# Three pieces of x moved from SyncE's DMA queue to ScalarE's at the start of a decoder block

## The chip, the cores and the metric

The kernel runs on one core of a Trainium2 chip. The time is the device time of one execution in microseconds (us), the median of several runs; less is better. A profile is one execution recorded by the hardware profiler. The engines are named as the profile names them: PE (TensorE matmuls, with its weight loads as PEld), DVE (VectorE), ACT (ScalarE), POOL (GpSimd) and SP (SyncE, which here only issues DMAs; its issues have the name SPq).

## The reference

One decoder block over 256 tokens of width 1024, in float32, in outline:

```python
u = rmsnorm(h, norm_mix_pre)
z = u @ w_in                      # 4096 columns: pool, q, k, v, two gates
y_pool = pool_mixer(p, pool_w, pool_scale) @ w_branch_pool
y_attn = moba_attention(q, k, v) @ w_branch_attn
m = sigmoid(g_pool) * y_pool + sigmoid(g_attn) * y_attn
h = h + rmsnorm(m @ w_out, norm_mix_post)
u2 = rmsnorm(h, norm_mlp_pre)
a = square(relu(u2 @ w_up))       # 4096 columns
h = h + rmsnorm(a @ w_down, norm_mlp_post)
```

What matters here is the very beginning: x has to be loaded and turned, and the first product that is made of it is the values, v = u @ w_in[:, 1536:2048].

## The kernel before, in words

Every float32 product is made of three matmuls (`mm3`, lines 232 to 234): each operand is split into a high part in fp32r and a low part, the rounding that is left, and high times high, low times high and high times low are summed in PSUM. So each block of a weight is first loaded raw (`Block.load`, line 80), then split: ACT copies it to the high part (`split_hi`, line 89), and DVE and POOL subtract to get the low part (line 93; `share_lo` gives DVE 352 of 512 columns and POOL 160). The order of the instructions on every engine is that of the program text; nothing reorders them.

The first stage makes the values. Its weight has eight pieces v_r of 128 rows and 512 columns (256 KB each), called piece 0 to piece 7 below; x has four pieces x(t, n) of 256 KB, where t is the half of the tokens (two halves of 128) and n the half of the 1024 columns. All are loaded over SP's queue, interleaved as line 202 and the lines behind it say:

```python
load_x(0, 0); g_mix.load(); load_v(0); load_v(1)
load_x(1, 0); load_v(2); load_x(0, 1); load_v(3); load_x(1, 1)
for k in range(4, KD): load_v(k)
```

PE turns a piece of x by four transposes (`turn_x`, line 322); ACT makes the high part uh of 128 columns of it (line 329) and DVE the low part ul (line 330). `v_rows(t, k)` is the three matmuls of piece k of the weight with half t of the tokens; there are 16 such triples. On PE they stand in this order: turn x(0,0), nine small matmuls that only keep the engine busy, v_rows(0,0), turn x(1,0), v_rows(0,1), v_rows(1,0), turn x(0,1), v_rows(1,1), v_rows(0,2), v_rows(1,2), turn x(1,1), and then the two halves of pieces 3 to 7. Piece 0 has its high part made by DVE (the CAST of line 375), pieces 1 to 7 by ACT.

Behind the values come q, k, the pool projection, the scores, the gates and the rest; their weights are all loaded over SP's queue, in three raw buffers.

ACT's first two instructions are the load of its function table and a one-column activation `warm` (line 67) that asks for it; then it waits for the first turned piece of x.

Of the kernel before, what the change touches and what calls it, by code (L numbers as in the profile page):

```python
# [16 lines left out]
P = 128  # L17
# [3 lines left out]
KD = D // P  # L21
# [12 lines left out]
def hybrid_block(ctx: ExitStack, tc: tile.TileContext, x, norm_mix_pre, w_in, b_gate, pool_w, pool_scale,  # L34
# [4 lines left out]
    nc = tc.nc  # L39
# [110 lines left out]
    def load_next():  # L150
        if done[0] < len(order):
            order[done[0]].load_all()
            done[0] += 1
# [12 lines left out]

    x_sb = act.tile([P, NT, D], F32, name="x_sb")

    def load_x(t, n):
        c = slice(n * 512, (n + 1) * 512)  # L170
        nc.sync.dma_start(x_sb[:, t, c], x[0, t * P:(t + 1) * P, c])


    class Columns:
# [24 lines left out]
    def load_v(k):  # L199
        bv[k // 4].load(k % 4)  # L200

    load_x(0, 0)
    g_mix.load()
    load_v(0)
    load_v(1)
    load_x(1, 0)
    load_v(2)
    load_x(0, 1)
    load_v(3)
    load_x(1, 1)  # L210
    for k in range(4, KD):
        load_v(k)
    load_next()
    others.load()

# [760 lines left out]
```

## Time and profile before

| | |
|---|---|
| median of 3 runs | 340.37 us (340.05 to 341.89) |
| the profiled execution's own time | 339.66 us |
| its span, from the first to the last instruction | 337.9 us |
| outside the span (339.66 less 337.9) | 1.76 us |
| PE busy | 329.9 us, 98% of the span |
| DVE, ACT, POOL busy | 220.3, 182.2 and 77.9 us |
| HBM read | 61.10 MB |

The time of an engine counts what it does, not whether anything waits for it. The chain of waits is followed back from the last instruction of the program, at each step to what released it; what lies on it set the end. All times of rows are counted from the start of the span.

### The profile page before, as it was taken

Reading aid. Unit: us, or ns where it says so; the run is one execution under the profiler, and the core shown is the slowest. Engines: PE = TensorE matmul, PEld = TensorE weight load, DVE = VectorE, ACT = ScalarE, POOL = GpSimd, SP = SyncE. Lnnn points to the kernel's source line nnn. Section 1 sums busy time; section 2 is a strip of 40 time slices with the busy share of each in tenths; the row PEclk is TensorE's granted clock in tenths of the full one; section 3 lists DMA queues with packets and bytes.
Section 4 is the critical chain, followed back from the end, with each engine's and each line's share of the span. In section 5 each row is a group of like instructions: output and inputs, shape, how many; then the busy total and the mean of one; then the engine's idle time right before and its main releaser. Section 6 shows DMA issues by size and latency. Waiting matters only on the chain.

```text
span 337.9 us, 5701 instructions
## 1 busy us (share of the span) xinstructions
PE 329.9 (98%) x2325; PEld 305.0 (90%) x2325; DVE 220.3 (65%) x292; ACT 182.2 (54%) x256; POOL 77.9 (23%) x68
## 2 busy tenths in 40 slices
PE   8999999999999999999999999999999999999992
PEld 7799999999999999888898998989989989899881
DVE  3899777998385789376686746637366374653535
ACT  3984678665837755175768436354263551544331
POOL 3698589155305000056600000000000000000000
PEclk9999999999999999999999999999999999999999
DMA  6996971644555946707355854907629267090003
GB/s 211 375 324 216 222 232 27 237 151 140 209 189 207 353 135 240 248 4 248 124 176 198 288 211 139 330 30 263 236 74 317 109 236 262 11 353 14 0 0 124
DMA packets 27363, 63.04 MB, mean 187 GB/s; under 512 B 1317, under 2 KB 2761, under 8 KB 27337
## 3 DMA queue, kind: packets, MB, share of 16 engines
q1 hardware_dynamic: 26760, 62.15, 53.4%
q0 software_dynamic: 576, 0.52, 1.2%
q8 instruction: 18, 0.29, 0.4%
q14 instruction: 9, 0.07, 0.1%
HBM read 61.10 MB, written 1.05 MB: 184 GB/s over the span
## 4 chain that ended last, share of the span: by engine, by line
PE 96%; DMA 1%; DVE 1%; SPq 0%; DVEq 0%; ACT 0%; issue 0%; ACTq 0%
PE up_ps L232 9%; PE up_ps L234 9%; PE up_ps L233 9%; PE d_ps L242 7%; PE d_ps L241 7%; PE d_ps L245 7%; PE g_ps L232 4%; PE g_ps L233 4%; PE g_ps L234 4%; PE wo_ps L241 2%; PE wo_ps L242 2%; PE wo_ps L245 2%; DMA x_sb<-in_x_dram 1%; PE q_ps L232 1%; PE p_ps L234 1%; PE q_ps L234 1%
## 5 line engine op out<-in xcount | busy, mean ns | idle before, releaser
L232 PE MATMUL up_ps<-u2h,up_h 128*128 128x256 f32 x224 | 62.1, 277 | 0.0
L233 PE MATMUL up_ps<-u2l,up_h 128*128 128x256 f32 x224 | 61.9, 276 | 0.0
L234 PE MATMUL up_ps<-u2h,up_l 128*128 128x256 f32 x224 | 61.9, 276 | 0.0
L93 DVE TENSOR_TENSOR dn_l<-dn_r,dn_h 128x2048 fp32r<-128x2048 f32 x16 | 36.5, 2292 | 16.4 <-ACT dn_h L89 16.3
L233 PEld LDWEIGHTS up_ps<-u2l,up_h 128*128 128x128 f32 x224 | 42.1, 188 | 0.0
L232 PEld LDWEIGHTS up_ps<-u2h,up_h 128*128 128x128 f32 x224 | 42.1, 188 | 0.0
L241 PE MATMUL d_ps<-dn_h,ah 128*128 128x512 f32 x108 | 42.1, 389 | 0.0
L242 PE MATMUL d_ps<-dn_l,ah 128*128 128x512 f32 x108 | 42.1, 389 | 0.0
L234 PEld LDWEIGHTS up_ps<-u2h,up_l 128*128 128x128 f32 x224 | 42.1, 188 | 0.0
L89 ACT ACTIVATE dn_h<-dn_r 128x2048 fp32r<-128x2048 f32 x16 | 30.4, 1915 | 21.2 <-issue 12.8
L892 POOL TENSOR_TENSOR o_out<-o_out,g_mlp_post 128x256 f32<-128x256 f32 x1 | 0.7, 737 | 159.1 <-ACT o_out L891 159.1
L232 PE MATMUL g_ps<-uh,g_h 128*128 128x256 f32 x128 | 35.6, 278 | 0.0
L93 DVE TENSOR_TENSOR up_l<-up_r,up_h 128x2048 fp32r<-128x2048 f32 (+1 forms) x14 | 30.2, 2193 | 8.1 <-ACT up_h L89 8.1
L233 PE MATMUL g_ps<-ul,g_h 128*128 128x256 f32 x128 | 35.3, 276 | 0.0
L234 PE MATMUL g_ps<-uh,g_l 128*128 128x256 f32 x128 | 35.3, 276 | 0.0
L245 PE MATMUL d_ps<-dn_h,al 128*128 128x512 f32 x108 | 33.2, 389 | 0.0
L805 ACT ACTIVATE relu<-up_ps 128x512 f32<-128x512 f32 x16 | 9.5, 597 | 39.4 <-PE up_ps L234 39.4
L89 ACT ACTIVATE up_h<-up_r 128x2048 fp32r<-128x2048 f32 x16 | 29.9, 1904 | 1.6 <-PE wo_ps L245 1.6
L807 DVE TENSOR_TENSOR a<-up_ps,relu 128x512 f32<-128x512 f32 x16 | 11.0, 690 | 28.9 <-ACT relu L805 28.8
L93 POOL TENSOR_TENSOR up_l<-up_r,up_h 128x640 fp32r<-128x640 f32 (+1 forms) x4 | 15.6, 3914 | 44.2 <-ACT up_h L89 44.2
L245 PEld LDWEIGHTS d_ps<-dn_h,al 128*128 128x128 f32 x108 | 20.3, 188 | 4.2
L233 PEld LDWEIGHTS g_ps<-ul,g_h 128*128 128x128 f32 x128 | 24.0, 188 | 0.0
(240 smaller groups left out, 858.0 us busy)
## 6 DMA issues: line engine op xcount, KB each, us to landing
up_r<-in_w_up_dram SPq DMA_DIRECT2D x16, 1024.0 KB, 5.6
dn_r<-in_w_down_dram SPq DMA_DIRECT2D x16, 1024.0 KB, 4.9
g_r<-in_w_in_dram SPq DMA_DIRECT2D x8, 1024.0 KB, 5.5
o_r<-in_w_out_dram SPq DMA_DIRECT2D x4, 1024.0 KB, 5.0
v_r<-in_w_in_dram SPq DMA_DIRECT2D x8, 256.0 KB, 5.4
q_r<-in_w_in_dram SPq DMA_DIRECT2D x4, 512.0 KB, 6.3
k_r<-in_w_in_dram SPq DMA_DIRECT2D x2, 1024.0 KB, 5.9
p_r<-in_w_in_dram SPq DMA_DIRECT2D x2, 1024.0 KB
```

The costliest lines, as they stand in the source:

```text
L89: nc.scalar.activation(self.hi[:, s, :], self.raw[:, s, :], AF.Copy)
L93: eng.tensor_tensor(self.lo[:, s, c], self.raw[:, s, c], self.hi[:, s, c].bitcast(F32), ALU.subtract)
L232: nc.tensor.matmul(ps, wh, rh, start=start, stop=False, skip_group_check=True)
L233: nc.tensor.matmul(ps, *second, start=False, stop=False, skip_group_check=True)
L234: nc.tensor.matmul(ps, *third, start=False, stop=stop, skip_group_check=True)
L241: nc.tensor.matmul(ps, xh, wh[:, c], start=start, stop=False, skip_group_check=True)
L242: nc.tensor.matmul(ps, xh, wl[:, c], start=False, stop=False, skip_group_check=True)
L245: nc.tensor.matmul(ps, xl, wh[:, c], start=False, stop=stop, skip_group_check=True)
L805: nc.scalar.activation(r, ps, AF.Relu)
L807: nc.vector.tensor_tensor(a, ps, r, ALU.mult)
L892: nc.gpsimd.tensor_tensor(o[:, 768:D], o[:, 768:D], g_mlp_post[:, 768:D], ALU.mult)
```

## The change

`load_x` is given the queue that it issues on. The first piece of x stays on SP's queue, the eight pieces of the weight follow it there without a break, and the other three pieces of x are issued by ACT, in the order x(1,0), x(0,1), x(1,1).

```diff
-    def load_x(t, n):
+    def load_x(t, n, queue):
         c = slice(n * 512, (n + 1) * 512)
-        nc.sync.dma_start(x_sb[:, t, c], x[0, t * P:(t + 1) * P, c])
+        queue.dma_start(x_sb[:, t, c], x[0, t * P:(t + 1) * P, c])
...
-    load_x(0, 0)
+    load_x(0, 0, nc.sync)
     g_mix.load()
-    load_v(0)
-    load_v(1)
-    load_x(1, 0)
-    load_v(2)
-    load_x(0, 1)
-    load_v(3)
-    load_x(1, 1)
-    for k in range(4, KD):
+    for k in range(KD):
         load_v(k)
+    for t, n in ((1, 0), (0, 1), (1, 1)):
+        load_x(t, n, nc.scalar)
     load_next()
     others.load()
```

Five lines fewer stand ahead of what follows, so a line of the kernel before has a number smaller by five after it (329 becomes 324).

SP's issues at the start of the program, before. x_sb are the pieces of x, v_r those of the weight; DMAHW0 to DMAHW7 are eight semaphores that the loads take in turn (x(0,0) has 0, g_mix 1, piece 0 has 2, piece 1 has 3, x(1,0) has 4, piece 2 has 5, x(0,1) has 6, piece 3 has 7), so that the ninth load waits until the first has landed.

```order
L80 DMA v_r<-in_w_in_dram 128x512 x2
L171 DMA x_sb<-in_x_dram 128x512
L80 DMA v_r<-in_w_in_dram 128x512
L171 DMA x_sb<-in_x_dram 128x512
L80 DMA v_r<-in_w_in_dram 128x512
L171 DMA x_sb<-in_x_dram 128x512 [waits DMAHW0_49]
L80 DMA v_r<-in_w_in_dram 128x512 [waits DMAHW1_49]
L80 DMA v_r<-in_w_in_dram 128x512 [waits DMAHW2_49]
L80 DMA v_r<-in_w_in_dram 128x512 [waits DMAHW3_49]
L80 DMA v_r<-in_w_in_dram 128x512 [waits DMAHW4_49]
L80 DMA q_r<-in_w_in_dram 128x2x512 [waits DMAHW5_49]
L80 DMA q_r<-in_w_in_dram 128x2x512 [waits DMAHW6_49]
```

The last two rows are the first two loads of q's weight. Pieces 4 to 7 are the four rows ahead of them.

The same place on SP after the change, where x(1,0), x(0,1) and x(1,1) hold the semaphores 3, 5 and 7, and pieces 1 to 4 hold 4, 6, 0 and 1:

```order
L171 DMA x_sb<-in_x_dram 128x512
L184 DMA g_mix_row<-in_norm_mix_pre_dram 8x128
L80 DMA v_r<-in_w_in_dram 128x512 x3
L80 DMA v_r<-in_w_in_dram 128x512 [waits DMAHW0_49]
L80 DMA v_r<-in_w_in_dram 128x512 [waits DMAHW1_49]
L80 DMA v_r<-in_w_in_dram 128x512 [waits DMAHW2_49]
L80 DMA v_r<-in_w_in_dram 128x512 [waits DMAHW3_49]
L80 DMA v_r<-in_w_in_dram 128x512 [waits DMAHW4_49]
L80 DMA q_r<-in_w_in_dram 128x2x512 [waits DMAHW5_49]
L80 DMA q_r<-in_w_in_dram 128x2x512 [waits DMAHW6_49]
```

Three issues have left SP; piece 3 now waits for x(0,0), piece 5 for piece 0, piece 6 for x(1,0) and piece 7 for piece 1.

ACT at the start of the program after the change, from its table load to the second weight piece that it splits:

```order
L67 ACT_TABLE_LOAD
L67 ACTIVATE warm<-eps 128x1 [waits DVE_49]
L171 DMA x_sb<-in_x_dram 128x512 x3
L324 ACTIVATE uh<-x_ps_164,g_mix_col 128x128 [waits DVE_49,PE_49]
L324 ACTIVATE uh<-x_ps_164,g_mix_col 128x128 [waits DVE_49]
L89 ACTIVATE v_h<-v_r 128x512 [waits DMAHW4_49]
L324 ACTIVATE uh<-x_ps_188,g_mix_col 128x128 [waits PE_49]
L324 ACTIVATE uh<-x_ps_188,g_mix_col 128x128 [waits DVE_49]
L89 ACTIVATE v_h<-v_r 128x512 [waits DMAHW6_49]
```

The three issues stand between `warm` and the first uh and wait for nothing of their own; the rest of ACT's order is as before.

## Rows read from the trace of the kernel before

**Rows 1.** The page: the span, and busy time, share and instructions of each engine.
```profile
span 337.9 us, 5701 instructions
...
PE 329.9 (98%) x2325; PEld 305.0 (90%) x2325; DVE 220.3 (65%) x292; ACT 182.2 (54%) x256; POOL 77.9 (23%) x68
```

**Rows 2.** The page: the chain that ended last, share of the span by engine.
```profile
PE 96%; DMA 1%; DVE 1%; SPq 0%; DVEq 0%; ACT 0%; issue 0%; ACTq 0%
```

**Rows 3.** The same chain in order of time, 0 to 20 us: start, length, what.
```profile
2.46 4.58 DMA x_sb<-in_x_dram
7.09 0.66 PE x_ps L322 x4
...
10.61 0.36 PE v_ps L233
...
12.33 0.23 PE v_ps L232
...
18.98 0.23 PE v_ps L234
```

**Rows 4.** Windows: stretch, then busy us of PE, PEld, DVE, ACT, POOL; clock, DMA share, GB/s.
```profile
1.50:2.00 0.50, 0.50 (x7) 0.50 (x6) 0.00 (x0) 0.50 (x1) 0.50 (x3) 1.00 0.27 102
0.00:3.35 3.35, 2.57 (x24) 2.48 (x24) 0.06 (x1) 1.49 (x2) 1.82 (x10) 1.00 0.39 119
5.00:6.00 1.00, 1.00 (x9) 0.68 (x7) 1.00 (x3) 0.58 (x3) 0.53 (x1) 1.00 0.90 285
12.00:13.00 1.00, 1.00 (x8) 0.86 (x6) 0.69 (x3) 0.63 (x2) 0.59 (x1) 1.00 1.07 410
20.00:330.00 310.00, 310.00 (x2219) 289.31 (x2218) 203.30 (x252) 167.02 (x224) 66.36 (x48) 1.00 0.53 181
```

**Rows 5.** Timeline of SP's issues: start, length, engine, line, what.
```profile
0.74 0.38 SPq L171 DMA_DIRECT2D x_sb<-in_x_dram  x1
2.46 0.43 SPq L171 DMA_DIRECT2D x_sb<-in_x_dram  x1
...
7.06 0.33 SPq L80 DMA_DIRECT2D v_r<-in_w_in_dram  x1
7.83 1.54 SPq L80 DMA_DIRECT2D q_r<-in_w_in_dram  x2
8.99 0.38 SPq L80 DMA_DIRECT2D q_r<-in_w_in_dram  x1
9.66 0.30 SPq L184 DMA_DIRECT2D others_row<-in_norm_mlp_pre_dram  x1
10.33 0.28 SPq L184 DMA_DIRECT2D others_row<-in_pool_scale_dram  x1
```

**Rows 6.** Timeline of ACT, 0 to 20 us.
```profile
2.03 0.20 ACT L67 ACTIVATE warm<-eps 128x1 f32<-128x1 f32 x1
4.78 0.37 ACT L329 ACTIVATE uh<-x_ps,g_mix_col 128x128 fp32r<-128x128 f32 x1 [2.55 <-PE x_ps L322]
...
5.83 0.62 ACT L89 ACTIVATE v_h<-v_r 128x512 fp32r<-128x512 f32 x1
...
15.70 3.93 ACT L89 ACTIVATE q_h<-q_r 128x1024 fp32r<-128x1024 f32 x4
```

**Rows 7.** Timelines of DVE, POOL and PE, 4.7 to 8.3 us, around pieces 0 and 1.
```profile
4.77 0.43 DVE L375 CAST v_h<-v_r 128x512 fp32r<-128x512 f32 x1 [0.86 <-DMA v_r<-in_w_in_dram]
...
6.53 0.86 POOL L93 TENSOR_TENSOR v_l<-v_r,v_h 128x160 fp32r<-128x160 f32 x1 [0.72 <-ACT v_h L89]
...
6.33 0.47 PE L234 MATMUL v_ps<-v_l,uh 128*128 128x512 f32 x1 [0.24 <-DVE v_l L93]
...
7.82 0.40 PE L233 MATMUL v_ps<-v_l,uh 128*128 128x512 f32 x1
```

**Rows 8.** The page's DMA issues: KB each, us to landing; POOL's own issues, in ns.
```profile
q_r<-in_w_in_dram SPq DMA_DIRECT2D x4, 512.0 KB, 6.3
...
L485 POOL DMA_DIRECT2D stacked<-stacked x4: 581/586/817, 32.3 to 36.2; - x4
```

## The prediction

> **What bounds the kernel now.** I read the page first: PE is busy for 98% of the span of 337.9 us [rows 1], and 96% of the chain that ended last is PE, 1% a DMA [rows 2]. So the question is what PE waits for, and where. The windows answer it: from 20 to 330 us PE is busy for 310.00 of 310.00 us [rows 4]. A delay or a gain ahead of 20 us therefore goes to the end undiminished, and nothing that happens to the transfers of x can save more than what PE loses before that.
>
> The chain in order of time shows the loss. It begins with the load of x(1,0), issued at 2.46 us, 4.58 us until it has landed at 7.04; PE turns it at 7.09 [rows 3]. From there it is PE without a hole, but for one matmul that took 0.36 us in place of 0.23 at 10.61; from 12.33 to the start of the last at 18.98 stand 30 matmuls at 0.23 each [rows 3]. PE had started the matmul before that wait at 6.33 [rows 7] and could have gone on 0.23 later, at 6.56. So at this place 7.09 - 6.56 = 0.53 us are to be had, with the 0.13 at 10.61 together 0.66 us: **0.2% of the time, the most that any order of landing gives** while piece 0 of the weight, at the head of its queue, lands at 4.77 [rows 7]. What can be lost has no such limit.
>
> I call "same" what lies within 0.5% of 340.37, that is 1.7 us; a measurement of this kernel can hardly tell less from no change. Durations come from the profiled execution, whose time of 339.66 us is 0.71 below the median; I add the differences to the median.
>
> **When the loads land now.** An issue on SP that waits for a semaphore shows when an earlier load landed. The issue at 7.06 waited for x(1,0), that at 7.83 for piece 2, at 8.99 for x(0,1), at 9.66 for piece 3, at 10.33 for x(1,1) [rows 5]; piece 0 landed at 4.77. Counting x(0,0) as the first, the second load landed at 4.77, the fourth at 7.04, the fifth to eighth at 7.83, 8.99, 9.66 and 10.33. Six loads of 256 KB in 5.56 us are 0.93 us each. The DMA engines are the limit here, at 285 GB/s and a share of 0.90 from 5 to 6 us; later they move 410 [rows 4].
>
> **The change, part by part.**
>
> *Three issues leave SP.* One takes 0.43 us [rows 5]. Piece 2 is issued where x(1,0) was, at 2.46, pieces 3 and 4 sooner than now as well. That alone is worth nothing, since it is the transfers that are slow, and not the issues.
>
> *Three issues come to ACT.* They start when `warm` is done, at 2.03 + 0.20 = 2.23 us, and ACT then stands idle until 4.78 [rows 6], 2.55 us. The trace has no issue on ACT. Its bounds are SP's 0.43 us and the longest of POOL's, 0.82 [rows 8]: 1.3 to 2.5 us for three. I take SP's, the same kind of transfer, so ACT is free at about 3.6; even the upper end ends at 4.7. Cost: nothing, covered by the idle time. Were the cover gone, the first uh would be late by as much as the issues run over, with 0.53 us of slack until x(1,0).
>
> x(1,0) is thus issued at about 2.26 and not 2.46: the table load and `warm` stand ahead of it, and the change **gains 0.2 us of issue, no more**. x(0,1) and x(1,1) gain more, but PE meets them without a wait now.
>
> *What lands when, with two queues.* This decides. x(0,0) was issued at 0.74 [rows 5] and its first bytes came after 1.5, at most 0.05 MB of them by 2.00 [rows 4], so at about 1.8: 1.1 us from issue to bytes. x(1,0), issued at 2.26, can move bytes from about 3.35. By then 119 GB/s x 3.35 us = 0.40 MB have been moved [rows 4], 1.5 loads: x(0,0) and half of piece 0. From there both queues have work all the time. If they share the engines evenly, loads end in this count of loads moved: piece 0 at 2.5 (it was 2), x(1,0) at 3.5 (it was 4), piece 1 at 4.5 (it was 3), x(0,1) at 5.5 (6), piece 2 at 6.5 (5), x(1,1) at 7.5 (8), piece 3 at 8 (7), and from piece 4 on all as before. Between the landings above this reads: piece 0 at 5.34, x(1,0) at 6.47, **piece 1 at 7.44**, x(0,1) 8.41, piece 2 9.33, x(1,1) 10.0, piece 3 10.33.
>
> The trace has nothing of two queues in this stage, so I bound the landing of piece 1: at the low end 5.83, when ACT starts on it now [rows 6], if the loads go on in the order of their issue; at the high end 8.99, as the sixth load, if all of x goes ahead of it. I take 7.44, the even share, which is also the middle.
>
> [...]
>
> *What PE then waits for.* Piece 0 at 5.34 moves the matmul at 6.33 to 6.90 and its end of turn to 7.13, level with the 7.09 of now; x(1,0) is there by then. But v_rows(0,1) needs piece 1 split. From the start of its high part on ACT (5.83) to the end of POOL's share of the low part (6.53 + 0.86 = 7.39) are 1.56 us [rows 6, 7], and the second matmul of that triple started at 7.82 [rows 7], 0.43 later. With piece 1 at 7.44 it starts at 7.44 + 1.56 = 9.00: **+1.18 us**. What is queued behind it on PE, v_rows(1,0), x(0,1) and v_rows(1,1), is ready by then. Piece 2, at 9.33, has its low part at about 10.9, and PE comes to it at about 11.3: no wait, and the 0.13 at 10.61 are saved. Piece 3 has nearly two microseconds to spare. Sum: 1.18 - 0.13 = **+1.05 us**, so 340.7 for the profiled execution and 341.4 as the median.
>
> *SP's later issues.* The first load of q's weight now waits for x(0,1), 8.41 in place of 7.83, and lands 6.3 us later [rows 8], at 14.7; ACT wants it at 15.70 [rows 6], or about a microsecond later now. Covered, by 1 us at least. The third is released by the low part of piece 3, which moves no more than PE does.
>
> **The rivals.**
>
> *Only the issue is saved* (B). The transfers keep the order of their issue, or the second queue fills the tenth of the engines' time that is idle from 5 to 6 us [rows 4] and makes good what piece 1 loses. For it: engines that reach 410 GB/s later have room at 285. [...] x(1,0) lands 0.2 sooner, at 6.84; PE gains 0.2 us, POOL's part at 7.39 allowing up to 0.43. Time: 340.2, between 339.7 (all of the 0.66) and 340.6.
>
> [...]
>
> *ACT's pieces go first* (C), the other side: slower. If the engines serve ACT's queue ahead of SP's, all three pieces of x are moved before piece 1, which lands as the sixth load at 8.99. Its low part is there at 8.99 + 1.56 = 10.55, and the matmul of 7.82 is late by 2.73; less 0.13, +2.6 us, 343.0. It counts as slower from 1.7 us on, when piece 1 lands after 7.82 + 0.13 + 1.7 - 1.56 = 8.1. For it: pieces of x wait in one queue, with no weight between them. Against: nothing in the rows sets one queue over another.
>
> *Not what it says* (D): ACT's issues late, by a table load that ends later or an issue that costs more than 0.82. Then x(1,0) takes over the wait again; each microsecond that it lands after 7.1 is one microsecond lost.
>
> **How the numbers follow.** Even share 0.53, its own range 340.4 to 342.1 (piece 1 between 6.4 and 8.1); B 0.33; C 0.10; D 0.02; a gain of over 0.5%, against the limit of 0.66 us, 0.02. The forecast is the likeliest, 341.4. The range is 339.7 to 342.7: it takes in B and the even share and leaves out C's point and what lies beyond. Faster by over 0.5%: 0.02. Slower: C 0.10, D 0.02, the upper tail of the even share 0.06, together 0.18. Same: 0.80.
>
> **What would show it.** Right: the chain of waits passes through piece 1, its high and low part, rather than the load of x(1,0); ACT starts on piece 1 at about 7.4; PE idles between the turned x(1,0) and v_rows(0,1); the matmuls from piece 3 on keep 0.23 us; from 20 us on PE is as full as now; ACT's three issues end before 4.7. Wrong: piece 1 split at 5.8 as now (B), or after 8.1 (C); x(1,0) still the wait; an idle PE behind 20 us, or a granted clock there below 1.00.

## The result and the profile after

The change made the kernel **slower: 343.37 us against 340.18, medians of six executions each, ratio 1.0096 [1.0078, 1.0115]**. That is +3.2 us where +1.05 was forecast, and it lies above the range.

The page of the changed kernel, its first lines and the chain of waits by engine:

```profile
span 340.7 us, 5701 instructions
...
PE 330.2 (97%) x2325; PEld 305.5 (90%) x2325; DVE 220.5 (65%) x292; ACT 182.1 (53%) x256; POOL 77.9 (23%) x68
...
PE 96%; DMA 2%; DVE 1%; SPq 0%; DVEq 0%; ACT 0%; issue 0%; ACTq 0%
```

The same work in a span longer by 2.8 us (337.9 in [rows 1]); the DMA's share of the chain has gone from 1% [rows 2] to 2%. The windows of the changed kernel say where those 2.8 us are. The columns are the stretch, its length, the busy time of PE, PEld, DVE, ACT and POOL, the granted clock of PE, the DMA engines' share and GB/s:

```profile
3.00:4.00 1.00, 0.50 (x5) 0.23 (x3) 0.00 (x0) 0.00 (x0) 0.00 (x0) 1.00 0.78 211
...
6.00:7.00 1.00, 0.00 (x0) 0.00 (x0) 0.00 (x0) 0.00 (x0) 0.00 (x0) 1.00 0.99 356
7.00:8.00 1.00, 0.12 (x1) 0.15 (x1) 0.69 (x3) 0.00 (x0) 0.18 (x1) 0.78 1.05 406
8.00:9.00 1.00, 1.00 (x3) 0.51 (x3) 0.98 (x2) 0.72 (x2) 0.34 (x1) 0.50 1.04 402
...
10.00:11.00 1.00, 1.00 (x5) 0.90 (x4) 0.07 (x1) 0.37 (x1) 0.22 (x1) 0.51 0.89 266
11.00:12.00 1.00, 1.00 (x5) 0.74 (x5) 0.57 (x2) 0.69 (x2) 0.00 (x0) 1.00 0.84 244
...
20.00:330.00 310.00, 310.00 (x2219) 289.11 (x2218) 203.67 (x246) 168.19 (x223) 68.45 (x49) 1.00 0.54 183
```

The same windows of the kernel before, for the stretch that matters:

```profile
3.00:4.00 1.00, 1.00 (x8) 0.78 (x7) 0.17 (x1) 0.00 (x0) 0.00 (x0) 1.00 0.87 231
...
6.00:7.00 1.00, 0.56 (x2) 0.19 (x1) 0.96 (x3) 0.46 (x1) 0.47 (x1) 1.00 0.79 248
7.00:8.00 1.00, 0.91 (x6) 0.87 (x7) 0.01 (x1) 0.21 (x1) 0.40 (x1) 1.00 0.84 266
8.00:9.00 1.00, 1.00 (x5) 0.49 (x4) 0.38 (x2) 0.58 (x3) 0.00 (x0) 1.00 0.82 295
```

From 6 to 7 us no engine of the changed kernel does anything, while the DMA engines are full (0.99). Then, at 7.88 us, the matmuls begin, but the clock column reads 0.78 from 7 to 8 us and 0.50 to 0.51 from 8 to 11, where the kernel before has 1.00. Behind 20 us PE is as full as in [rows 4]. PE had also stood still from 3.50 to 4.65, for the 4 KB load of g_mix (start, length, what; in brackets the idle time ahead and what ended it):

```profile
4.65 0.20 PE L189 MATMUL g_mix_ps<-ident,g_mix_row 8*128 8x8 f32 x1 [1.15 <-DMA g_mix_row<-in_norm_mix_pre_dram]
```

The chain in order of time names what all engines waited for (start, length, what):

```profile
1.58 5.70 DMA v_r<-in_w_in_dram
7.30 0.44 DVE v_h L370
7.88 0.76 PE v_ps L227
8.64 0.43 PE v_ps L228
9.07 0.57 PE v_ps L229
9.64 0.85 PE x_ps L317 x4
10.49 0.43 PE v_ps L227
10.92 0.32 PE v_ps L228
11.23 0.23 PE v_ps L229
...
21.80 0.23 PE v_ps L229
```

It is **piece 0 of the weight**: issued at 1.58 us, landed at 7.28. In the kernel before it had landed at 4.77 [rows 7], and the chain began with x(1,0) [rows 3]. From 11.23 on every matmul of the values takes 0.23 or 0.24 us again; the last of the values starts at 21.80, 2.82 later than the 18.98 of [rows 3], and this is the whole loss in the span. Why piece 0 is late stands in ACT's timeline (start, length, engine, line, what; in brackets the idle time ahead and what ended it):

```profile
0.74 1.28 ACT L67 ACT_TABLE_LOAD   x1 [0.74 <-PEq L957]
0.91 1.35 ACTq L171 DMA_DIRECT2D x_sb<-in_x_dram  x3
2.03 0.20 ACT L67 ACTIVATE warm<-eps 128x1 f32<-128x1 f32 x1
5.47 0.37 ACT L324 ACTIVATE uh<-x_ps,g_mix_col 128x128 fp32r<-128x128 f32 x1 [3.23 <-PE x_ps L317]
8.65 0.63 ACT L89 ACTIVATE v_h<-v_r 128x512 fp32r<-128x512 f32 x1 [0.26 <-DMA v_r<-in_w_in_dram]
```

ACT issued its three loads **from 0.91 us on, while its table load ran (0.74 to 2.02) and before `warm` (2.03)**, though both stand ahead of them in its program. "Nothing reorders them", as it stands ahead of the prediction, holds for the program text and not for what ACT did with it. So x(1,0) and x(0,1) went out right behind x(0,0) (0.74) and ahead of piece 0 (1.58), x(1,1) at 1.8. The DMA view of the changed kernel, from 3 to 4.5 us, shows whose bytes then moved (q1 is SP's queue, q10 ACT's; packets, MB, share of the 16 engines):

```profile
q10 hardware_dynamic: 195, 0.36, 75.8%
q1 hardware_dynamic: 29, 0.03, 10.4%
```

and the same view from 4.5 to 6 us:

```profile
q1 hardware_dynamic: 130, 0.24, 59.3%
q10 hardware_dynamic: 99, 0.18, 34.2%
```

### The profile page after: what moved, and what is told of

It is laid out like the page before. It is cut to its first block, busy times and chain, and to the rows that moved or that the text cites. A ratio compares the mean times of both kernels' runs of the same rounds, so it can differ in the third digit from the quotient of the medians.

```text
span 340.7 us, 5701 instructions
## 1 busy us (share of the span) xinstructions
PE 330.2 (97%) x2325; PEld 305.5 (90%) x2325; DVE 220.5 (65%) x292; ACT 182.1 (53%) x256; POOL 77.9 (23%) x68
## 3 DMA queue, kind: packets, MB, share of 16 engines
HBM read 61.10 MB, written 1.05 MB: 182 GB/s over the span
## 4 chain that ended last, share of the span: by engine, by line
PE 96%; DMA 2%; DVE 1%; SPq 0%; DVEq 0%; ACT 0%; issue 0%; ACTq 0%
PE up_ps L227 9%; PE up_ps L229 9%; PE up_ps L228 9%; PE d_ps L237 7%; PE d_ps L236 7%; PE d_ps L240 7%; PE g_ps L228 4%; PE g_ps L227 4%; PE g_ps L229 4%; PE wo_ps L236 2%; PE wo_ps L237 2%; PE wo_ps L240 2%; DMA v_r<-in_w_in_dram 2%; PE v_ps L227 1%; PE v_ps L228 1%; PE v_ps L229 1%
```

## The experiments

All are made from the changed kernel, and the diffs are against it. The kernel before ran beside them, with medians 339.81 us beside e1, e2, e3 and e5, 340.06 beside e6 to e9, and 339.98 beside e10 to e12. The theory after the result: ACT's early issue put bytes that PE needs late ahead of piece 0, and the hole that this made in PE's work (5.95 to 7.88 us) cost the clock as well. The rivals: a second queue is in itself dear; the clock alone is the loss.

**e1: the three issues held back.** One ACT copy into a column of x(1,0), which the load overwrites, makes ACT's loads wait for an instruction that ends at 2.33 us. This makes the prediction's assumption true.

```diff
+    nc.scalar.activation(x_sb[:, 1, 0:1], eps, AF.Copy)
     load_x(0, 0, nc.sync)
```

> Theory (the time of ACT's issues decides): ACT's queue issues the three pieces of x at 0.91 us, under the table load, so piece 0 of the weight shares the engines with x(1,0) and x(0,1) and lands fourth. Here they wait for an ACT instruction behind warm, so the first is issued at about 2.4: piece 0 lands between 4.8 and 5.4, piece 1 at about 7.2, the granted clock stays 1.00, time 340.4 to 341.6 (ratio to before 1.001 to 1.004). Rival (a second queue costs by itself, whenever it is used, because it is served ahead): piece 0 still lands after 6.5, 342.5 or more.

Measured: 340.68 us, 1.0030 [1.0015, 1.0045]. ACT's timeline of this kernel:

```profile
2.14 0.19 ACT L202 ACTIVATE x_sb<-eps 128x1 f32<-128x1 f32 x1
2.35 1.37 ACTq L171 DMA_DIRECT2D x_sb<-in_x_dram  x3
```

DVE starts on piece 0 at 4.88 us, near the 4.77 of [rows 7]. So about two thirds of the loss are the early issue (0.42 to 0.90 of the 0.96%, by the two intervals). The median is what the prediction's sum gave (1.05 of 340 is 1.0031), but the profile does not show its mechanism: in the profiled execution, the fastest of the nine at 339.47 us, ACT split piece 1 at 5.87, and the second matmul of v_rows(0,1) started at 7.49, earlier than before. Of the nine executions three had a mean granted clock of 0.988 to 0.990 and took 341.49 to 341.81; the others, at 0.994 to 0.997, took 339.47 to 340.85.

**e9: the same with eight more small matmuls** that keep PE busy while it waits for piece 0.

```diff
+    nc.scalar.activation(x_sb[:, 1, 0:1], eps, AF.Copy)
     load_x(0, 0, nc.sync)
...
-    keep_busy(9)
+    keep_busy(17)
```

> The held version (ACT's issues behind an ACT instruction, at 2.35) with 17 in place of 9 matmuls that keep PE busy until piece 0 is there. Theory (the held version's slower runs, 341.5 to 341.8 at a granted clock of 0.988 to 0.990, come from the hole of 0.69 us ahead of piece 0): all runs between 339.3 and 340.0, ratio to before 0.998 to 1.000. Rival (the spread comes from where the loads land): the spread stays at 2 us and the ratio at 1.003.

Measured: 340.43 us, 1.0016 [1.0006, 1.0027], so the loss did not vanish as I had expected, and the spread is 1.5 us (340.01 to 341.54); but no execution's clock was under 0.994. Here the profile does show the predicted chain:

```profile
1.99 4.91 DMA v_r<-in_w_in_dram
...
6.91 0.64 ACT v_h L89
...
7.62 0.87 POOL v_l L93
...
8.53 0.50 PE v_ps L229
```

Piece 1 lands at 6.9, is split, and the second matmul of v_rows(0,1) waits for POOL's share until 8.53. The prediction had 7.44 and 9.00. The last of the values starts at 19.55, 0.57 later than in [rows 3], and the median is 0.16% or 0.5 us up.

**e3: the order in which an even share would finish, all on SP's queue**: x(1,0) and x(0,1) ahead of piece 0, x(1,1) behind it, no second queue.

```diff
     g_mix.load()
-    for k in range(KD):
+    load_x(1, 0, nc.sync)
+    load_x(0, 1, nc.sync)
+    load_v(0)
+    load_x(1, 1, nc.sync)
+    for k in range(1, KD):
         load_v(k)
-    for t, n in ((1, 0), (0, 1), (1, 1)):
-        load_x(t, n, nc.scalar)
```

> All on SP's queue, in the order in which an even share of the two queues would finish: x(0,0), x(1,0), x(0,1), piece 0, x(1,1), pieces 1 to 7. Theory (only the order of the bytes counts): piece 0 lands fourth, at about 7.0, piece 1 sixth, at about 9.0, and the time is that of the changed kernel, 342.5 to 343.8. Rival (two queues in use are the cost, the order little): below 341.5.

Measured: 343.64 us, 1.0102 [1.0082, 1.0122], the loss of the change itself. DVE's timeline:

```profile
6.50 0.43 DVE L372 CAST v_h<-v_r 128x512 fp32r<-128x512 f32 x1 [2.60 <-DMA v_r<-in_w_in_dram]
```

A second queue is not needed for the loss; the order is enough. The way there is not quite the same: piece 0 is 0.8 us earlier here than in the change, and g_mix was in time (3.43).

**e2 and e8: the clock kept up.** e2 has 30 small matmuls for 9 behind the turn of x(0,0); e8 also has 36 for 24 at the start of the program.

```diff
-    keep_busy(24)
+    keep_busy(36)
...
-    keep_busy(9)
+    keep_busy(30)
```

> The changed kernel with 30 in place of 9 matmuls that only keep PE busy ahead of piece 0. Theory (the late piece 0 is the loss, the clock an addition): piece 0 lands at 7.3 as in the changed kernel, the granted clock stays 1.00 from 7 to 11 us where it was 0.50, and 0.4 to 0.8 us are saved: about 342.8. Rival (the clock is the loss): the time falls to 340.2 to 341.

> The changed kernel with PE kept busy in both of its holes (36 in place of 24 matmuls at the start, 30 in place of 9 behind x(0,0)). Theory: piece 0 still lands at 7.0 to 8.3; the matmuls of 512 columns follow each other in 0.23 us from v_rows(0,0) on, where they took 0.43 in the changed kernel; ratio to before 1.005 to 1.008 (the changed kernel 1.0096), so the clock is a fourth to a half of the loss. Rival (the clock is nearly all of it): ratio below 1.003.

e2: 342.17 us, 1.0068 [1.0056, 1.0080]. It says nothing on the clock alone: PE stood idle from 3.5 to 4.67 us all the same, waiting for g_mix, and the matmuls of the first triple were still 0.43 to 0.57 apart until 9.9, the spacing that the change has in the windows at 0.50 above. (The clock column of e2 reads 1.00 there, as does that of e6 and e7 below. That the clock was low in e2, e6, e7 and e10 is my estimate from the spacing alone.) e8 filled that hole too: 342.02 us, 1.0061 [1.0046, 1.0076]. PE's timeline of e8:

```profile
5.19 1.92 PE L61 MATMUL busy<-const-bfloat16-1.0 128*128 128x128 bf16 x30
8.38 0.48 PE L227 MATMUL v_ps<-v_h,uh 128*128 128x512 f32 x1 [1.27 <-DVE v_h L370]
8.70 0.40 PE L228 MATMUL v_ps<-v_h,ul 128*128 128x512 f32 x1
```

and the last of the values in its chain:

```profile
21.83 0.23 PE v_ps L229
```

The first two matmuls are 0.32 apart at once, where the change had 0.56 (7.88 to 8.44), and the clock column reads 1.00 from 8 to 9 us, though piece 0 is later still (its split starts at 7.81, 0.51 behind the change's). What is left, 1.96 us, is the late piece 0 for the most part. The difference to the change, 1.0096 less 1.0061, is 1.2 us by the medians (0.4 to 2.0 by the two intervals), but the two profiles show **about 0.5 us for the clock**: from the first matmul of the values to the last are 13.92 us in the change (7.88 to 21.80) and 13.45 here. The last of the values starts no earlier here; what makes this span 0.5 us shorter lies behind the values and is not explained.

**e6, e7 and e12: one piece alone on ACT's queue**, with the loads on SP in the order of the kernel before. The diff is e6's; in e7 `nc.scalar` stands with x(1,1) instead, in e12 with x(0,1).

```diff
-    for k in range(KD):
+    load_v(0)
+    load_v(1)
+    load_x(1, 0, nc.scalar)
+    load_v(2)
+    load_x(0, 1, nc.sync)
+    load_v(3)
+    load_x(1, 1, nc.sync)
+    for k in range(4, KD):
         load_v(k)
-    for t, n in ((1, 0), (0, 1), (1, 1)):
-        load_x(t, n, nc.scalar)
```

> The kernel before with x(1,0) alone on ACT's queue, the rest in its old order on SP. Theory (issue at 0.91 and even share): x(0,0) and x(1,0) end together as first and second load, piece 0 is third and lands at about 5.8 where it was 4.8, piece 1 fourth at about 7.0, so the second matmul of v_rows(0,1) starts at about 8.6 where it was 7.8: 0.5 to 1.2 us slower (ratio 1.0015 to 1.0035), a third of the changed kernel's loss. Rival (the wait for x(1,0) was the bound, and it is gone): 0.2 to 0.5 us faster.

> The kernel before with x(1,1) alone on ACT's queue, the piece of x that PE wants last. Theory: it is issued at 0.91 all the same and goes ahead of piece 0, which lands third at about 5.8; then piece 1 fourth, x(1,0) fifth at about 7.8, so PE turns x(1,0) at about 7.8 where it was 7.1: 0.6 to 1.2 us slower. Rival (a piece that nobody waits for costs nothing): same time within 0.3 us.

> x(0,1) alone on ACT's queue, not held; compare with x(1,0), 1.0063, and x(1,1), 1.0017. If the cost of x(1,0) comes from its moving beside x(0,0), whose rows lie 0.5 MB ahead of its own, x(0,1) moves as fast as x(1,1) did, 0.6 loads in half a microsecond, and the ratio is 1.001 to 1.003. If it is the place in the order that counts, x(0,1) costs between the two, 1.003 to 1.005.

| on ACT's queue | time, us | ratio | split of piece 0 starts |
|---|---|---|---|
| e6: x(1,0) | 342.22 | 1.0063 [1.0049, 1.0078] | 7.11 |
| e7: x(1,1) | 340.54 | 1.0017 [1.0007, 1.0027] | 5.07 |
| e12: x(0,1) | 340.33 | 1.0005 [0.9988, 1.0021] | 5.27 |

The splits are of one execution each; e7's was the slowest of its twelve, e12's the fastest. All three pieces are issued at 0.91 us, ahead of piece 0, and should by my theory have delayed it by the same one load of 0.93 us. x(1,1) and x(0,1) delayed it by 0.3 and 0.5 at most, x(1,0) by 2.3. The times hold more than this delay: in e6 the matmuls of the values are 0.43 apart until 12 us, the spacing of the change at 0.50, and in e7 0.42 to 0.58 until 9.6; in e7 PE also waited for x(1,0) until 8.30 (7.09 in [rows 3]). e12 came out below both of its expectations, nearer the first. The DMA view from 3 to 4.5 us, of e6:

```profile
DMA packets 160, 0.27 MB, mean 178 GB/s; under 512 B 24, under 2 KB 32, under 8 KB 160
```

and of e7:

```profile
DMA packets 322, 0.55 MB, mean 369 GB/s; under 512 B 46, under 2 KB 54, under 8 KB 322
```

With x(1,1) the engines move twice the bytes in the same 1.5 us, enough to make room for one load more (e12: 0.52 MB). The kernel before, with one queue, moved 0.38:

```profile
q1 hardware_dynamic: 206, 0.38, 84.9%
```

So the loss comes with x(1,0) in particular. It is tempting to say that x(1,0) and x(0,0) move slowly side by side, but x(0,0) was nearly in by then: from 0 to 3 us SP's queue of e6 moved 0.26 MB, which is its size, and from 3 to 4.5 us what moved on SP's queue beside x(1,0) was mainly g_mix and piece 0 (the first row is from 0 to 3 us, the others from 3 to 4.5):

```profile
q1 hardware_dynamic: 141, 0.26, 26.0%
...
q10 hardware_dynamic: 90, 0.16, 37.2%
q1 hardware_dynamic: 70, 0.11, 33.3%
```

No run shows what kept SP's queue back behind x(0,0). In this window it moved 0.11 MB in e6, 0.03 in the change, and 0.15 in e10 (below), where piece 0 was first on ACT's queue, but 0.31 in e7 and 0.34 in e12.

**e11: x(1,0) alone, and held back as in e1.**

> x(1,0) alone on ACT's queue, but held behind an ACT instruction until about 2.35; compare with x(1,0) alone and not held, 1.0063. Theory (the time of issue is the cause): piece 0 lands by 5.2, x(1,0) by 7.0, ratio 0.9985 to 1.0015. Rival (x(1,0) on another queue costs by itself): ratio above 1.004.

Measured: 341.44 us, 1.0033 [1.0009, 1.0058], from 339.71 to 342.95, between what I had expected and the rival. Piece 0 was in time (5.12), but PE waited for x(1,0), as this row of its timeline shows:

```profile
8.08 1.11 PE L323 MATMUL x_ps<-ident,x_sb 128*128 128x128 f32 x4 [0.92 <-DMA x_sb<-in_x_dram]
```

Issued at 2.36, it had landed a microsecond later than before, where it had been issued at 2.46, and behind the wait, from 8.85 to 11.12, the matmuls of the values were 0.42 to 0.57 apart; the mean granted clock of this execution was 0.989. The place on the second queue brought no earlier landing here.

**e5 and e10: piece 0 moved to ACT's queue**, to turn the early issue to use: in e5 with the three pieces of x behind it there, in e10 alone, with x on SP's queue in the order of before.

```diff
-        def load(self, k=0):
+        def load(self, k=0, queue=None):
...
-            nc.sync.dma_start(self.raw[:, k:k + self.by, :], self.w[
+            (queue or nc.sync).dma_start(self.raw[:, k:k + self.by, :], self.w[
...
+    load_v(0, nc.scalar)
```

> Piece 0 of the weight goes first on ACT's queue, then the three pieces of x. Theory (even share in the order of issue): x(0,0) and piece 0 land together as first and second, piece 0 by 5.0, then piece 1 and x(1,0) as third and fourth, by 7.0; no clock loss; 339.8 to 341.0. Rival (ACT's queue is served ahead): piece 0 lands before x(0,0), and piece 1 after 8.0; 341.5 or more.

> Piece 0 alone on ACT's queue, everything else in its old order on SP. Theory (what is issued at 0.91 goes into the stream beside x(0,0), and both queues together move more than one): x(0,0) and piece 0 are what PE needs first, so nothing is overtaken; piece 0 lands by 4.8, the queue behind has one load less and x(1,0) lands at 6.3 to 7.0; ratio to before 0.9985 to 1.0005. Rival (a second queue in use at the start delays SP's queue, x(0,0) and g_mix too): g_mix lands after 4.3, PE starts on x(0,0) a microsecond late, ratio above 1.001.

e5: 341.21 us, 1.0037 [1.0025, 1.0049], a little above what I had expected. Piece 0 is there by 4.95, but x(1,0) comes at 7.74 and piece 1 at 7.9. e10: 340.86 us, 1.0013 [0.9989, 1.0036], no difference that can be told. There g_mix's 4 KB, second on SP's queue, reached PE only at 5.29 us, and with it the whole start was late, as the rival had said. In every kernel of the study whose ACT issued a load at 0.91 (the change, e2, e5 to e8, e10, e12) g_mix came late, at 4.2 to 5.3 us; in the others it was there when PE was first free, at 3.43. No kernel of the study was faster than the one before.

## Why the prediction was wrong

*The failed step* is one sentence, "They start when `warm` is done, at 2.23 us". The issues began at 0.91, and the sum followed from the wrong start. I had read ACT's timeline as one row of work in program order; the row of the trace shows three loads that wait for nothing issued past work that ACT had in hand. With 0.91 in its place ACT's bytes would have begun at about 2.0, and the prediction's own count would have put x(1,0) and nearly all of x(0,1) ahead of piece 0, which then ends at 3.8 to 4 loads moved: 6.8 to 7.0 by the landings of [rows 5]. It landed at 7.28. I had counted piece 0 as 0.57 late; it was 2.5 late, and PE had nothing to do without it. Piece 1, which the prediction looked at, was split from 8.65, where it had 7.44 and called anything past 8.1 wrong. e1 undoes the step alone and takes the loss from 0.96% to 0.30%; e3 reproduces it on one queue.

*A term that was missing* is the clock. The prediction looked for a lower clock behind 20 us and priced none ahead of it. PE was idle from 3.50 to 4.65 us (g_mix's 4 KB stand second on SP's queue and reached PE at 4.65) and again from 5.95 to 7.88, and the clock stood at 0.50 to 0.51 from 8 to 11. By the medians of e8 and the change this is 1.2 us of 3.2 (0.4 to 2.0), by their profiles 0.5; most of the rest is the late piece 0.

*The even share of the two queues* did not hold in the change. It was an estimate of mine that no run shows as a rule, and the 7.44 for piece 1, and with it the term of +1.18, rested on it; the runs showed piece 1 split from 8.65 in the change, 5.87 in e1 and 6.91 in e9. ACT's queue moved 0.36 MB against SP's 0.03 from 3 to 4.5 us, and 0.18 against 0.24 from 4.5 to 6. In e1, with the issues at 2.35 as the prediction had them, the share was about even from 4.5 to 6 us (0.25 against 0.22), but ACT's queue had moved only 0.01 MB before that, where the prediction had it moving from 3.35; so piece 0 was hardly late. And the pieces together did not keep one rate: 0.27 MB or 0.55 in the same 1.5 us, by which piece of x stood on ACT's queue (e6, e7). The count of loads at 0.93 us each, on which every landing of the prediction rested, could not know this.

*Rival C* (ACT's pieces first, 343.0) came nearest in time, and ACT's bytes did go first for a while. Its place was wrong: not piece 1 as the sixth load but piece 0 was what PE lacked, and ACT's pieces were issued first, from 0.91 us on, against 1.58 for piece 0.

*Right* were: PE behind 20 us is full, so that the delay ahead of it reached the end undiminished (2.82 us at the last matmul of the values, 2.8 in the span; in e2, e6, e8 and e11, though, the stretch behind that matmul was 0.5 us shorter, 318.4 against 318.9); ACT's issue costs about what SP's does (three take 1.35 us, 0.45 each, where SP's takes 0.43) and lies in ACT's idle time; and the chain now passes through a piece of the weight in place of x(1,0), though through piece 0 and not piece 1. That SP's fewer issues are worth nothing no run shows by itself; that no more than 0.66 us was to be gained fits the runs, none of which gained. With the issues at 2.3 us, as the prediction had them, the time is 1.0030 (e1) where its sum gave 1.0031. That is luck in part: three of e1's nine executions ran at a lower clock, its profile does not pass through piece 1, and where a profile does, in e9 (1.0016), the term of +1.18 is 8.53 - 7.82 = 0.71.

*Open* are why SP's queue is held back behind x(0,0) when x(1,0) or piece 0 is first on ACT's (0.11, 0.03 and 0.15 MB from 3 to 4.5 us in e6, the change and e10), and less with x(1,1) or x(0,1) (0.31 and 0.34 in e7 and e12), what the 0.30% of e1 is beyond e9's part of it, and why executions of one kernel (e1, e11) differ by 2.3 and 3.2 us. All were seen, none was explained.

## What to carry to other kernels

Before a load is moved to another engine's queue, ask when that queue will issue it and whose bytes it will then overtake; here loads that waited for nothing went out at 0.91 us, past a table load and an activation that stood ahead of them on their engine. Where the order matters, keep the loads on one queue, or give the load something real to wait for, as the one-column copy of e1 (0.30% still stayed lost). The hole in TensorE's work at the start of the program was paid twice in the change: once for the wait (some 2 us), and once for the matmuls at a granted clock of 0.50 behind it (0.5 to 1.2 us, estimated from e8 and the change). Not every hole was: in e8 PE was idle for 1.27 us, and the matmuls behind it were 0.32 apart.

## What the runs showed of the hardware

- ACT issued three DMAs from 0.91 to 2.26 us while its own table load (0.74 to 2.02) was running.
- The two queues did not share evenly in the change: ACT's moved 0.36 MB against SP's 0.03 from 3 to 4.5 us, then 0.18 against 0.24. In e1 it was 0.25 against 0.22 from 4.5 to 6.
- Where ACT issued a load at 0.91 us, g_mix's 4 KB, second on SP's queue, reached PE at 4.2 to 5.3 us; elsewhere by 3.43.
- The rate from 3 to 4.5 us differed with the piece that stood on ACT's queue: 178 GB/s with x(1,0), 369 with x(1,1); 254 with one queue, before.
- The engines of the change moved more a little later (356 and 406 GB/s from 6 to 8 us, before 248 and 266), but the bytes that PE waited for were not the first among them. That it was the second queue is not shown: e6 moved 366 there with SP's queue alone.
